# A streamed LoRA matmul: idle matmuls around TensorE's loop, a pause that waits on another store, and other chunk sizes

## The chip, the core and the metric

The kernel runs on one core of a Trainium2 chip. The metric is device time in microseconds of one execution; three runs of the kernel before gave 162.35 to 162.37, with a median of 162.37. A separate profiled execution gives the trace. Its numbers are used for everything that is read inside the kernel, and its own time is given beside its span.

The engines' short names are: PE for TensorE's matmuls, PEld for its weight loads, DVE for VectorE, ACT for ScalarE, POOL for GpSimd, SP for the SyncE queue that issues most of the transfers here.

## The reference

`x` is 16 x 2048 x 256 in float32, that is 32,768 rows of 256. `W` is 256 x 256, `lora_A` 256 x 16, `lora_B` 16 x 256, `lora_E` has 16 values.

```python
x_flat = x.reshape(-1, in_dim)
y = x_flat @ W
lora_out = x_flat @ lora_A
lora_out = lora_out * lora_E
lora_out = lora_out @ lora_B
y = y + scale * lora_out
```

Reading `x` and writing the output are 33.55 MB each.

## The kernel before

The kernel folds the low-rank part into the weights once: `weff = W + A * E * scale @ B`, in bf16 (L149 to L167). After that it is one matmul of 32,768 rows with a 256 x 256 matrix.

**Chunks and slots.** The 256 rows of 128 partitions (one "row" below is 128 rows of `x`, 131,072 bytes) are cut into six chunks by `PLAN`: 48, 32, 48, 48, 48 and 32. A partition holds consecutive rows of `x`, so that a whole chunk is one contiguous run for each partition. Four slots in SBUF (`SLOTS`) hold a chunk each; a chunk is loaded into its slot, computed there, and its result is written over it in place and stored from it. Chunk 4 goes into chunk 0's slot and chunk 5 into chunk 1's. `PIECES` splits a chunk's load into several transfers, so that work can start on the first of them: chunk 0 into 16 and 32 rows, chunk 2 into 24 and 24.

**The transfers.** All large transfers are issued by SP, in program order: load 0's first piece, W, the rest of load 0, loads 1 to 3 (L114 to L121); then, from the loop at L210, store 0 and store 1 as soon as their chunks are computed. Behind store 1 (`AFTER`), SP waits until store 0 has landed and issues load 4, waits until store 1 has landed and issues load 5. Then come stores 2 to 5, each when its chunk is done. As SP works in order, store 2 can't be issued ahead of load 5.

**Steps.** A step is eight rows, and there are 32 (`NS`). For each step, VectorE rounds the rows to bf16 (`rounded`, L141); TensorE transposes them, two bf16 values taken as one fp32 word (`transposed`, L180); VectorE copies the transposed words from PSUM to SBUF (`copied`, L145); TensorE multiplies by `weff` in two halves of eight matmuls (`multiplied`, L191); ScalarE copies each half from PSUM into the slot (L214). All buffers between the engines are double. The orders are written out by hand: VectorE does `copied(t)` and then `rounded(t + 2)`; TensorE's loop (L201) transposes step t + 1 and then multiplies step t. So the last multiplication of a chunk comes after the first transposition of the next chunk.

**Waits.** `rounded` waits for the load that brings its rows (L135). `HOLD = {3: 1}` adds a wait at chunk 3's first step, step 16: after ten no-operations on VectorE, rounding waits until store 1 has landed (L140). Step 15's multiplication stands behind the transposition of step 16 on TensorE, and so chunk 2's last rows wait for that too.

Of the kernel before, what the change touches and what calls it, by code (L numbers as in the profile page):

```python
# [3 lines left out]

PLAN = [48, 32, 48, 48, 48, 32]

PIECES = {0: [16, 32], 2: [24, 24]}

SLOTS = [48, 32, 48, 48]
LEAD = 4  # L10
AFTER = {1: [4, 5]}

HOLD = {3: 1}

S, G = 8, 4
P = 128
# [17 lines left out]
def kernel(tc, x, W, lora_A, lora_B, lora_E, scale, out):  # L34
    nc = tc.nc
# [5 lines left out]
    KC = K // P  # L41
    assert K == M and sum(PLAN) * P == N
    starts = [sum(PLAN[:i]) * P for i in range(len(PLAN))]

    steps = [(i, r) for i, b in enumerate(PLAN) for r in range(0, b, S)]
    NS = len(steps)
    assert NS % 2 == 0

    def rows_of(flat, i):
        b, r0 = PLAN[i], starts[i]  # L50
        return flat[r0:r0 + b * P, :].rearrange("(p b) k -> p b k", b=b)

    def sbuf(name, shape, dt):
        return nc.alloc_sbuf_tensor(name, shape, dt).ap()

    def psum(name, shape, dt):
        return nc.alloc_psum_tensor(name, shape, dt).ap()

    slots = [sbuf(f"xy{s}", [P, rows, K], FP32) for s, rows in enumerate(SLOTS)]
    a_sb = sbuf("a_sb", [P, KC, R], FP32)  # L60
# [4 lines left out]
    ate = sbuf("ate", [R, KC, P], BF16)  # L65
    weff = sbuf("weff", [P, KC, M], BF16)
    ident = sbuf("ident", [P, P], FP32)

    xb = [sbuf(f"xb{k}", [P, S, K], BF16) for k in range(2)]
    words = [t[:, :, :].rearrange("p s k -> p (s k)").bitcast(FP32).rearrange("p (s w) -> p s w", s=S) for t in xb]  # L70
# [4 lines left out]
    ps_y = [psum(f"psum_y{k}", [P, G, M], FP32) for k in range(2)]  # L75
# [4 lines left out]
    s_w, s_a, s_b, s_e = (Count(nc, f"s_{k}") for k in "wabe")  # L80

    pieces = {}
    for i, b in enumerate(PLAN):
        parts = PIECES.get(i, [b])
        pieces[i] = [(sum(parts[:j]), n) for j, n in enumerate(parts)]
    s_ld = {(i, r): Count(nc, f"s_ld{i}_{r}") for i in pieces for r, n in pieces[i]}
    s_st = [Count(nc, f"s_st{i}") for i in range(len(PLAN))]
    s_id, s_set, s_v, s_t, s_m, s_y = (
        Count(nc, k) for k in ("s_id", "s_set", "s_v", "s_t", "s_m", "s_y"))


    can_m = nc.alloc_semaphore("can_m")
# [1 line left out]
    can_y = [[nc.alloc_semaphore(f"can_y{h}_{k}") for k in range(2)] for h in range(S // G)]  # L94

    def slot(i):
        return slots[i % LEAD][:, :PLAN[i], :]
# [8 lines left out]
    def spent(engine, count):  # L106
        engine.wait_ge(count.sem, count.total).then_inc(count.sem, -count.total)

    def take(sem):
        nc.tensor.wait_ge(sem, 1).then_inc(sem, -1)  # L110
# [21 lines left out]
    def rounded(t):  # L132
        i, r = steps[t]
        if (i, r) in s_ld:
            nc.vector.wait_ge(s_ld[i, r].sem, 16)  # L135
        if i in HOLD and r == 0:

            for _ in range(10):
                nc.vector.engine_nop()
            nc.vector.wait_ge(s_st[HOLD[i]].sem, 16)  # L140
        nc.vector.tensor_copy(out=xb[t % 2], in_=slot(i)[:, r:r + S, :]).then_inc(can_t[t % 2], 1)  # L141

    def copied(t):
        nc.vector.wait_ge(s_t.sem, t + 1)
        nc.vector.tensor_copy(out=xt[t % 2], in_=ps_xt[t % 2]).then_inc(can_m, 1)  # L145


    nc.vector.wait_ge(s_b.sem, 16)
# [3 lines left out]
    for c in range(KC):  # L152
# [4 lines left out]
    s_v.by(nc.vector.tensor_scalar(  # L157
        out=ate, in0=ps_at, scalar1=e_sb, scalar2=float(scale),
        op0=mybir.AluOpType.mult, op1=mybir.AluOpType.mult))
    nc.tensor.wait_ge(s_v.sem, 2)  # L160
    for c in range(KC):
        aeb_done = nc.tensor.matmul(ps_aeb[:, c, :], ate[:, c, :], b_bf, start=True, stop=True)  # L162
    s_set.by(aeb_done)
    rounded(0)
    nc.vector.wait_ge(s_w.sem, 16)
    nc.vector.wait_ge(s_set.sem, 2)
    s_v.by(nc.vector.tensor_add(out=weff, in0=w_sb, in1=ps_aeb))  # L167
    rounded(1)
    for t in range(NS):
        copied(t)  # L170
        if t + 2 < NS:
            rounded(t + 2)

    nc.vector.sem_inc(can_t[NS % 2], 1)


    def transposed(k):
        nc.tensor.wait_ge(can_t[k], 1)
        for j in range(S):
            done = nc.tensor.transpose(ps_xt[k][:, j, :], words[k][:, j, :], ident)  # L180
            if j == 1:
                done.then_inc(can_t[k], -1)
        done.then_inc(s_t.sem, 1)

    def multiplied(k):
        take(can_m)
        for h in range(S // G):
            nc.tensor.wait_ge(can_y[h][k], 1)
            for j in range(G):
                for c in range(KC):  # L190
                    done = nc.tensor.matmul(  # L191
                        ps_y[h][:, j, :], pairs[k][:, h * G + j, :, c], weff[:, c, :],
                        start=(c == 0), stop=(c == KC - 1))
                if j == 0:
                    done.then_inc(can_y[h][k], -1)
            done.then_inc(s_m.sem, 1)

    transposed(0)
    nc.tensor.wait_ge(s_v.sem, 3)

    with nc.tensor.Fori(0, NS // 2):  # L201
        for k in range(2):
            transposed(1 - k)
            multiplied(k)
    s_t.total, s_m.total = NS + 1, NS * S // G

    for h in range(S // G):
# [1 line left out]
    n = 0  # L209
    for i, r in [(i, r + g) for i, r in steps for g in range(0, S, G)]:  # L210
        n += 1
        nc.scalar.wait_ge(s_m.sem, n)
        t, h = divmod(n - 1, S // G)
# [16 lines left out]
    for count in [s_a, s_id]:  # L230
        spent(nc.tensor, count)
    spent(nc.tensor, s_v)
    for count in [s_b, s_e, s_w, s_set, s_t] + list(s_ld.values()):
        spent(nc.vector, count)
    spent(nc.scalar, s_m)
    nc.tensor.wait_ge(can_y[0][NS % 2], 1).then_inc(can_y[0][NS % 2], -1)
# [37 lines left out]
```

## Time and profile before

| | us |
|---|---|
| median of three runs | 162.37 |
| the profiled execution's own time | 162.57 |
| its span, first to last instruction | 161.3 |
| outside the span | 1.27 |
| first rounding (step 0) starts | 9.60 |
| rounding waits for load 0's second piece until | 19.58 |
| stores 0 to 5 issued at | 37.21, 47.69, 91.12, 107.07, 122.79, 133.27 |
| loads 4 and 5 issued at | 73.68, 83.38 |
| TensorE's pause | 59.68 to 84.67 |
| last engine work (ScalarE's copy) ends | 133.2 |

How to read it: a page of the profile gives the busy time of each engine over the whole span, then forty equal slices with the busy share in tenths. The DMA row is the mean busy share of the core's 16 DMA engines, and the GB/s row what they moved; the packets of this kernel are up to 48 KB long, so that short windows of the rate are coarse. PEclk is TensorE's granted clock; 1.00 is the full clock and 0.50 half of it. The table of stages gives the same for stretches that one chooses. A transfer is issued by a short instruction on its queue; the time from there to landing holds both its wait behind the transfers ahead and its own movement.

### The profile page before, as it was taken

What the parts mean: (1) busy time and instruction counts of PE and PEld (TensorE: products, weight loads), DVE (VectorE), ACT (ScalarE), POOL (GpSimd) and SP (SyncE); (2) the same over time, 40 slices, a digit from 0 to 9 for tenths busy, and PEclk for the clock granted to TensorE, in tenths of its full rate; (3) what the DMA queues carried; (4) which work ended last, traced back from release to release, by engine and by line L of the source; (5) the groups of instructions that cost most, each with busy time, mean ns of one, the idle gap of its engine ahead of it and who ended that gap; (6) DMA issues with size and microseconds to landing.
All of it is one profiled execution on the core that took longest, in us unless ns stands there. A gap on an engine that the chain in (4) does not pass through costs nothing.

```text
span 161.3 us, 1875 instructions
## 1 busy us (share of the span) xinstructions
PE 93.2 (58%) x780; PEld 83.4 (52%) x780; DVE 76.6 (48%) x67; ACT 63.2 (39%) x65; POOL 0.7 (0%) x6
## 2 busy tenths in 40 slices
PE   0149179999999980000009999999999970000000
PEld 0038058999999960000008899999999960000000
DVE  0074197898989800000039589898989500000000
ACT  0300406777768680000000577776868680000000
POOL 0100000000000000000000000000000000000000
PEclk9999978999999998555555899999999997555555
DMA  4999999999999999989999989999999999999993
GB/s 137 407 496 423 423 423 433 408 463 408 506 439 427 402 390 392 500 386 398 480 435 402 500 378 406 471 431 404 463 463 415 402 451 463 427 402 402 447 447 171
DMA packets 2370, 67.42 MB, mean 418 GB/s; under 512 B 432, under 2 KB 448, under 8 KB 576
## 3 DMA queue, kind: packets, MB, share of 16 engines
q1 hardware_dynamic: 2160, 67.37, 97.7%
q10 hardware_dynamic: 208, 0.03, 0.1%
q14 instruction: 2, 0.02, 0.0%
HBM read 33.85 MB, written 33.55 MB: 418 GB/s over the span
## 4 chain that ended last, share of the span: by engine, by line
PE 44%; DMA 22%; ACT 2%; DVE 1%; issue 0%
PE psum_y L191 29%; DMA out_dram<-xy 22%; PE psum_xt L180 14%; ACT xy L214 2%; DVE xb L141 1%
## 5 line engine op out<-in xcount | busy, mean ns | idle before, releaser
L214 ACT COPY xy<-psum_y 128x1024 f32<-128x1024 f32 x64 | 61.9, 1015 | 64.0 <-PE psum_y L191 64.0
L191 PE MATMUL psum_y<-weff,xt 128*128 128x256 bf16 x512 | 64.9, 283 | 0.1
L191 PEld LDWEIGHTS psum_y<-weff,xt 128*128 128x128 bf16 x512 | 51.8, 101 | 7.6 <-issue 0.3
L141 DVE CAST xb<-xy 128x2048 bf16<-128x2048 f32 x32 | 39.0, 1217 | 32.3 <-DMA out_dram<-xy 26.8
L180 PE MATMUL psum_xt<-ident,xb 128*128 128x128 f32 x264 | 37.1, 288 | 29.7 <-DVE xb L141 29.7
L180 PEld LDWEIGHTS psum_xt<-ident,xb 128*128 128x128 f32 x264 | 32.3, 150 | 31.3 <-DVE xb L141 30.9
L145 DVE COPY xt<-psum_xt 128x1024 f32<-128x1024 f32 x32 | 39.2, 1224 | 11.2 <-PE psum_xt L180 11.2
L153 PE MATMUL psum_xt<-ident,a_sb 128*16 128x128 f32 x2 | 0.6, 397 | 6.8 <-POOL ident L127 6.8
L149 DVE CAST b_bf<-b_sb 16x256 bf16<-16x256 f32 x1 | 0.3, 281 | 7.9 <-DMA b_sb<-in_lora_B_dram 7.9
L214 ACT ACT_TABLE_LOAD x1 | 1.3, 1283 | 6.0 <-PEq L123 6.0
L153 PEld LDWEIGHTS psum_xt<-ident,a_sb 128*16 128x16 f32 x2 | 0.1, 90 | 6.7 <-DMA a_sb<-in_lora_A_dram 6.7
L162 PE MATMUL psum_xt<-b_bf,ate 16*128 16x256 bf16 x2 | 0.6, 402 | 2.4 <-DVE ate L157 2.4
L162 PEld LDWEIGHTS psum_xt<-b_bf,ate 16*128 16x128 bf16 x2 | 0.1, 104 | 2.9 <-DVE ate L157 2.9
L157 DVE TENSOR_SCALAR ate<-psum_xt,e_sb 16x256 bf16<-16x256 f32 x1 | 0.5, 473 | 1.0 <-DMA e_sb<-in_lora_E_dram 1.0
L167 DVE TENSOR_TENSOR weff<-w_sb,psum_xt 128x512 bf16<-128x512 f32 x1 | 0.7, 669 | 0.0
L127 POOL TENSOR_SCALAR_AFFINE_SELECT ident<-ident 128x128 f32<-128x128 f32 x1 | 0.3, 292 | 0.2 <-POOL ident L125 0.2
L125 POOL MEMSET ident<- 128x128 f32 x1 | 0.2, 205 | 5.4 <-POOLq L123 5.4
L255 POOL MEMSET const-bfloat16-1.0<- 128x1 bf16 x1 | 0.1, 102 | 0.0
L255 POOL MEMSET const-uint8-127<- 128x1 uint8 x1 | 0.1, 101 | 0.0
L255 POOL MEMSET const-float32-0.0<- 128x1 f32 x1 | 0.1, 98 | 0.2 <-issue 0.2
L255 POOL MEMSET const-float32-1.0<- 128x1 f32 x1 | 0.1, 98 | 0.0
## 6 DMA issues: line engine op xcount, KB each, us to landing
out_dram<-xy SPq DMA_DIRECT2D x4, 6144.0 KB, 30.6
xy<-in_x_dram SPq DMA_DIRECT2D x3, 4096.0 KB, 24.5
xy<-in_x_dram SPq DMA_DIRECT2D x2, 6144.0 KB, 39.3
out_dram<-xy SPq DMA_DIRECT2D x2, 4096.0 KB, 31.8
xy<-in_x_dram SPq DMA_DIRECT2D x2, 3072.0 KB, 36.7
xy<-in_x_dram SPq DMA_DIRECT2D x1, 2048.0 KB, 8.4
w_sb<-in_W_dram SPq DMA_DIRECT2D x1, 256.0 KB, 8.5
a_sb<-in_lora_A_dram ACTq DMA_DIRECT2D x1, 16.0 KB, 5.7
```

The costliest lines, as they stand in the source:

```text
L127: s_id.by(nc.gpsimd.affine_select(out=ident, in_=ident, compare_op=mybir.AluOpType.not_equal, fill=1.0, base=0, pattern=[[-1, P]], channel ...
L141: nc.vector.tensor_copy(out=xb[t % 2], in_=slot(i)[:, r:r + S, :]).then_inc(can_t[t % 2], 1)
L145: nc.vector.tensor_copy(out=xt[t % 2], in_=ps_xt[t % 2]).then_inc(can_m, 1)
L149: s_v.by(nc.vector.tensor_copy(out=b_bf, in_=b_sb))
L153: at_done = nc.tensor.transpose(ps_at[:, c, :], a_sb[:, c, :], ident)
L157: s_v.by(nc.vector.tensor_scalar(out=ate, in0=ps_at, scalar1=e_sb, scalar2=float(scale), op0=mybir.AluOpType.mult, op1=mybir.AluOpType.mult))
L162: aeb_done = nc.tensor.matmul(ps_aeb[:, c, :], ate[:, c, :], b_bf, start=True, stop=True)
L167: s_v.by(nc.vector.tensor_add(out=weff, in0=w_sb, in1=ps_aeb))
L180: done = nc.tensor.transpose(ps_xt[k][:, j, :], words[k][:, j, :], ident)
L191: done = nc.tensor.matmul(ps_y[h][:, j, :], pairs[k][:, h * G + j, :, c], weff[:, c, :], start=(c == 0), stop=(c == KC - 1))
L214: y = nc.scalar.copy(out=slot(i)[:, r:r + G, :], in_=ps_y[h])
L255: nc = _bacc.Bacc("TRN2", target_bir_lowering=False, num_devices=1)
```

## The change

- `PLAN` becomes 48, 40, 40, 48, 48, 32, and the slots follow. Chunk 0 is loaded in two pieces of 24 rows, chunk 2 in one piece.
- The pause moves from chunk 3's first step (step 16) to its second (step 17), and waits for store 0 instead of store 1. There VectorE then raises a semaphore, `go`, and waits for another, `s_warm`, before it rounds.
- TensorE's loop of 16 iterations becomes an outer loop of two with an inner one of eight (16 steps). After each inner loop, TensorE waits for `go` and for a free `psum_y`, issues five idle matmuls and raises `s_warm`. The second time is after the last step, where VectorE raises `go` at the end of its work.
- One idle matmul is put ahead of the low-rank matmuls, two ahead of the first step. An idle matmul multiplies the fp32 identity with a broadcast of itself, 512 columns, into `psum_y[0]`, which nobody reads in that state.

```diff
-PLAN = [48, 32, 48, 48, 48, 32]
-PIECES = {0: [16, 32], 2: [24, 24]}
-SLOTS = [48, 32, 48, 48]
+PLAN = [48, 40, 40, 48, 48, 32]
+PIECES = {0: [24, 24]}
+SLOTS = [48, 40, 40, 48]
 LEAD = 4
 AFTER = {1: [4, 5]}
-HOLD = {3: 1}
+HOLD = 0
+WARM = 1, 2, 5
...
+    wide = ident[:, :].unsqueeze(1).to_broadcast([P, 4, P])
...
-        if i in HOLD and r == 0:
+        if t == NS // 2 + 1:
             for _ in range(10):
                 nc.vector.engine_nop()
-            nc.vector.wait_ge(s_st[HOLD[i]].sem, 16)
+            nc.vector.wait_ge(s_st[HOLD].sem, 16)
+            nc.vector.sem_inc(go, 1)
+            nc.vector.wait_ge(s_warm.sem, 1)
         nc.vector.tensor_copy(out=xb[t % 2], in_=slot(i)[:, r:r + S, :]).then_inc(can_t[t % 2], 1)
...
+    def idle(n):
+        for _ in range(n):
+            last = nc.tensor.matmul(ps_y[0][:, :2, :].rearrange("p g m -> p (g m)"), ident, wide, start=True, stop=True)
+        return last
...
+    idle(WARM[0])
     nc.tensor.wait_ge(s_v.sem, 2)
     for c in range(KC):
         aeb_done = nc.tensor.matmul(ps_aeb[:, c, :], ate[:, c, :], b_bf, start=True, stop=True)
...
     nc.vector.sem_inc(can_t[NS % 2], 1)
+    nc.vector.sem_inc(go, 1)
...
+    idle(WARM[1])
     transposed(0)
     nc.tensor.wait_ge(s_v.sem, 3)
-    with nc.tensor.Fori(0, NS // 2):
-        for k in range(2):
-            transposed(1 - k)
-            multiplied(k)
+    with nc.tensor.Fori(0, 2):
+        with nc.tensor.Fori(0, NS // 4):
+            for k in range(2):
+                transposed(1 - k)
+                multiplied(k)
+        take(go)
+        nc.tensor.wait_ge(can_y[0][0], 1)
+        idle(WARM[2]).then_inc(s_warm.sem, 1)
+    s_warm.total = 2
```

More of the change, by code (lines that the diff above doesn't have):

```diff
@@ L46 @@
     NS = len(steps)
-    assert NS % 2 == 0
+    assert NS % 4 == 0
     def rows_of(flat, i):
@@ L87 @@
     s_st = [Count(nc, f"s_st{i}") for i in range(len(PLAN))]
-    s_id, s_set, s_v, s_t, s_m, s_y = (
-        Count(nc, k) for k in ("s_id", "s_set", "s_v", "s_t", "s_m", "s_y"))
+    s_id, s_set, s_v, s_t, s_m, s_y, s_warm = (
+        Count(nc, k) for k in ("s_id", "s_set", "s_v", "s_t", "s_m", "s_y", "s_warm"))
+    go = nc.alloc_semaphore("go")
     can_m = nc.alloc_semaphore("can_m")
@@ L232 @@
     spent(nc.tensor, s_v)
-    for count in [s_b, s_e, s_w, s_set, s_t] + list(s_ld.values()):
+    for count in [s_b, s_e, s_w, s_set, s_t, s_warm] + list(s_ld.values()):
         spent(nc.vector, count)
```

## The prediction

> **What bounds the kernel now.** I read the table of engines first, then the 40 slices, the chain of waits, rates by stage, and the queue's own timeline.
>
> ```profile
> PE 93.2 (58%) x780; PEld 83.4 (52%) x780; DVE 76.6 (48%) x67; ACT 63.2 (39%) x65; POOL 0.7 (0%) x6
> ...
> PEclk9999978999999998555555899999999997555555
> DMA  4999999999999999989999989999999999999993
> ...
> DMA packets 2370, 67.42 MB, mean 418 GB/s; under 512 B 432, under 2 KB 448, under 8 KB 576
> ...
> PE 44%; DMA 22%; ACT 2%; DVE 1%; issue 0%
> ```
>
> No compute engine is busy for 60% of the span. The DMA row has a 9 in nearly every slice but the first and the last. The chain gives TensorE 44%, and that line misleads: it follows semaphores, and a transfer that lies in a queue behind other transfers shows none. The next view, busy time and rate by stage (start:end, length, busy time of PE, PEld, DVE, ACT and POOL, granted clock, DMA share, GB/s), decides it:
>
> ```profile
> 2.00:10.00 8.00, 0.86 (x4) 0.25 (x4) 1.08 (x3) 1.28 (x1) 0.50 (x2) 1.00 1.04 405
> 10.00:54.00 44.00, 39.17 (x320) 34.78 (x319) 34.38 (x31) 23.64 (x25) 0.00 (x0) 0.96 1.01 435
> 54.00:59.00 5.00, 5.00 (x48) 4.67 (x47) 2.31 (x2) 3.62 (x5) 0.00 (x0) 1.00 0.88 344
> 59.00:82.00 23.00, 0.68 (x7) 0.36 (x4) 0.00 (x0) 1.76 (x2) 0.00 (x0) 0.59 1.03 443
> 82.00:106.00 24.00, 21.33 (x170) 19.25 (x171) 19.31 (x17) 12.54 (x13) 0.00 (x0) 0.83 0.99 427
> 106.00:133.00 27.00, 26.15 (x240) 24.07 (x238) 19.56 (x17) 20.07 (x22) 0.00 (x0) 1.00 1.00 431
> 133.00:158.80 25.80, 0.00 (x0) 0.00 (x0) 0.00 (x0) 0.24 (x1) 0.00 (x0) 0.53 0.99 429
> 158.80:161.30 2.50, 0.00 (x0) 0.00 (x0) 0.00 (x0) 0.00 (x0) 0.00 (x0) 0.50 0.09 39
> ```
>
> From 2 us to 158.8 us the transfers run at 427 to 443 GB/s, whether the engines work (106 to 133) or stand still (59 to 82, 133 to 158.8). One dip stands out, 344 GB/s at 54 to 59, where the first four loads end and the first store begins. The last engine work ends at 133.2, and 28 us of stores follow. So the time is bytes over rate, plus ragged ends: 67.42 MB at 435 GB/s is 155.0 us, the first packet moves at 2.0 us, and some 4 us go to the slow start, the dip and the last, uneven 2.5 us. Whether engine work can matter is a matter of when the next transfer is queued:
>
> ```profile
> 0.94 0.38 SPq L101 DMA_DIRECT2D xy<-in_x_dram  x1
> 1.38 0.44 SPq L115 DMA_DIRECT2D w_sb<-in_W_dram  x1
> 1.87 2.95 SPq L101 DMA_DIRECT2D xy<-in_x_dram  x5
> 37.21 10.82 SPq L104 DMA_DIRECT2D out_dram<-xy  x2
> 73.68 10.04 SPq L101 DMA_DIRECT2D xy<-in_x_dram  x2
> 91.12 42.48 SPq L104 DMA_DIRECT2D out_dram<-xy  x4
> ...
> DMA to landing us min/median/max: 28.0/30.6/36.5
> ```
>
> The last line is of the six stores. A store of 6.29 MB needs 14.5 us at 435 GB/s, and the shortest took 28.0 us from issue: each lay at least 13 us behind others.
>
> **The change, part by part.** The profiled execution took 162.57 us: span 161.3 and 1.27 outside. The median of the plain runs is 162.37, 0.20 less. Sizes are in rows: one row of a chunk over 128 partitions is 131,072 bytes, 0.301 us at 435 GB/s. As a check, store 1 (32 rows) landed 9.7 us after store 0, by the waits that ended at 73.68 and 83.36; 32 x 0.301 = 9.6.
>
> *Chunks.* Bytes and order of the transfers stay. Landings in the changed kernel, estimated from rows: load 0 at 19.6 as now (where rounding waited for it), load 1 at 31.6, load 2 at 43.7, load 3 at 58.2, store 0 at 73.7 as now, store 1 (now 40 rows) at 85.7, load 4 at 100.2, load 5 at 109.8, store 2 at 121.9, store 3 at 136.4, store 4 at 150.9, store 5 at 160.5. The sixteen engines issue one load fewer, 128 packets. In the trace's packet records (which no view prints) packets of the first loads follow each other on an engine every 613 ns at 16 KB, 912 at 24, 1,214 at 32, 1,816 at 48, where 37.75 ns a KB would give 604, 906, 1,208, 1,812. So a packet costs some 4 to 9 ns by itself, and eight fewer on each engine, with the 16 KB ones gone, save 0.03 to 0.1 us. I take 0.1.
>
> *First piece 24 rows, not 16.* It lands 8 x 0.301 = 2.4 us later, so the first rounding moves from 9.60 to about 12.0, and W behind it by as much. Hidden: three steps instead of two then run before the next piece lands at 19.6, and store 0, issued at 37.2 now, comes not later than that; the queue needs it at 58.2, 20 us after.
>
> *Idle matmuls, 1 and 2 ahead of the first step.* No row has a plain fp32 matmul. By fp32 transposes (eight of 128 columns in 0.87 us at full clock, 1.57 to 1.97 at half) 512 columns cost 0.44 to 1.0 us; at double the passes, 0.87 to 2.0. I take 1.7 at half clock. The first lies between 7.4 and 9.7, where TensorE waits. The two others start at 10.3 and end by 13.7, against data ready at 13.2: at most 0.5 us (1.1 at the upper end), covered by the same 20 us. The Trainium skill's "FP8 and Floating Point Precision" (section "TensorE Precision Notes") gives true fp32 four passes; that is the upper price.
>
> *The pause.* Rounding 16 stays ahead of it, so chunk 2 is finished about 64, not 91; store 2 is queued by SP behind load 5 in any case, at 85.7 instead of 91.1, and is needed at 109.8. The wait now is on store 0 (73.7) and then on five idle matmuls, 2.2 to 10 us, so rounding 17 starts at 76 to 84 against 83.4 for rounding 16. Behind it on VectorE stands everything else, copy 16 among it. Five steps at 2.62 us (the spacing of the copies in the steady stretch) plus a start of some 3 us finish chunk 3 by 92 to 100; store 3 is needed at 121.9. Then step 22 must wait for load 4 until 100.2, a stall that takes the place of part of the pause. From there 10 steps are left: 16 steps with a cold start took 83.4 to 133.3, so 49.9 - 6 x 2.62 = 34.2 us, end at 134.4; store 4, four steps earlier, at 123.9. They are needed at 136.4 and 150.9: slack of 12 and 16 us, against 11.9 and 16 now. On the path: nothing.
>
> *Whether the clock is kept.* The clock by stage in the present pause:
>
> ```profile
> 61.00:63.00 2.00, 0.00 (x0) 0.00 (x0) 0.00 (x0) 0.00 (x0) 0.00 (x0) 1.00 1.13 492
> 63.00:65.00 2.00, 0.00 (x0) 0.00 (x0) 0.00 (x0) 0.00 (x0) 0.00 (x0) 0.50 1.16 496
> 65.00:84.00 19.00, 0.00 (x0) 0.00 (x0) 0.62 (x1) 0.00 (x0) 0.00 (x0) 0.50 1.00 433
> 84.00:90.30 6.30, 5.63 (x27) 4.64 (x28) 5.15 (x5) 1.23 (x2) 0.00 (x0) 0.50 0.94 406
> ```
>
> TensorE stopped at 59.7 and was at half clock from 63; the restart stayed there until 90.3. The Trainium skill's "TensorE: Matmul & The Clock Gate" (section "Why this matters for your kernels") says that an idle gap over some 3 us brings the half clock back; the trace agrees, 3.3 us here. By that rule the change defeats itself: what five matmuls warm is cold again in the wait for load 4. Without the page: any idle time of 3.3 us or more before 100.2 does it, and the 34.2 us above already hold a cold start.
>
> *Outer loop, go, s_warm.* Two branches and two waits, under 1 us on TensorE inside that slack. The idle matmuls after the last step run beside stores.
>
> Sum: 162.57 - 0.1 = 162.5 for the profiled execution, and 162.37 - 0.1 = 162.3 for the median.
>
> **Rivals.**
> A: TensorE is the path after all, as the 44% says. For: that line. A warm clock would then save, after the pause, 1.97 - 0.87 and 3.41 - 1.75, and at 21 to 26 us 3.53 - 1.75, about 4.5 us, giving 157.9. Against: 2.0 + 155.0 + the 0.5 from the last packet to the span's end + 1.27 is 158.8 without any of it. Chance 2%.
> B, faster: the end is set by the slowest of sixteen DMA engines. By the packet records they end between 158.9 and 160.7, mean 159.5; the late ones lost 0.3 to 1.4 us on their first packet, 0.1 to 1.0 in the dip, and up to 0.7 once at 64. A different first piece redraws the start. If the last engine came halfway to the mean: 162.37 - 0.6 = 161.8. Chance 18%.
> C, slower: engine work beside stores. One DMA engine's 48 KB packets took 93 to 126 ns longer from 106 to 133, beside stores 2 and 3, and no longer beside loads or in rest. In the changed kernel steps 17 to 21 run beside store 1. If they and the idle matmuls cover all 12 us of it, that is 6.3 packets' worth at 0.11 = 0.7 us more on that engine, less 0.1 for a shorter stretch later: 162.9. It decides if that engine ends last in plain runs too and work starts by about 78. Against: the mean rates with and without work are 431 and 429 GB/s. The Trainium skill's "SBUF — State Buffer" (section "SBUF: two separate sides") says that a DMA can't be slowed by a compute operation; then C would be nothing. Chance 20%.
> D, slower: the queue runs dry because a wait is longer than I think. Store 4 would have to be 12 us late; each microsecond beyond adds one: 163.5 or more. Chance 5%.
>
> **How the numbers follow.** About 0.2% (0.3 us) is what a measurement of this kernel tells from no change. The forecast, 162.3, has 55%. Faster by more than that: A and B, 20%. Slower: C and D, 25%. Its own range is 162.0 to 162.6. The range reaches to B's end where the slowest engine comes to 0.8 below its present time, 161.6, and to C's full price, 163.0; A, D and the tails of B lie outside.
>
> **What would show it.** Right: the DMA row full from slice 2 on, last engine work between 130 and 136 with 25 us or more of stores behind it, landing minus own time above 9 us for every store, a second pause of TensorE ending near 100 with its clock at half again. Right in part: rounding 17 between 76 and 84. Wrong: a hole in the DMA row at 58, 86, 110, 122, 136 or 151; a dip at the first store much smaller or larger than 344 GB/s over 5 us; or rates beside store 1 below 425 GB/s.

## The result

The changed kernel took 163.15 us (median of 22 runs, 162.69 to 163.51), the kernel before 162.51 in the 22 runs beside it (162.29 to 163.14; the three runs shown earlier lay at the low end of these). The ratio is 1.0035, with a 95% interval of 1.0024 to 1.0045: 0.35% slower, clear of no change. The profiled execution took 163.45 us, span 162.1.

The page of the changed kernel, busy time and slices:

```profile
PE 107.8 (66%) x806; PEld 87.7 (54%) x806; DVE 75.9 (47%) x67; ACT 63.1 (39%) x65; POOL 0.7 (0%) x6
...
DMA  5999999999999989989899998999999998999992
...
DMA 39%; PE 22%; ACT 2%; DVE 1%; issue 0%
...
L156 PE MATMUL psum_y<-ident 128*128 128x512 f32 x26 | 17.5, 828 | 10.6 <-PEq L114 10.3
```

TensorE is 14.6 us busier. The idle matmuls (L156, two records each) take 17.5 us, and the rest of its work 2.9 us less than before; its mean granted clock is 0.871, where it was 0.822. The DMA row is as full as before. The stages (start:end, length, busy time of PE, PEld, DVE, ACT, POOL, granted clock, DMA share, GB/s), cut as before:

```profile
2.00:10.00 8.00, 2.14 (x4) 0.66 (x4) 0.21 (x1) 1.28 (x1) 0.50 (x2) 1.00 0.97 382
10.00:54.00 44.00, 40.16 (x324) 34.44 (x324) 34.74 (x33) 23.47 (x25) 0.00 (x0) 1.00 1.02 440
54.00:59.00 5.00, 5.00 (x48) 4.67 (x46) 2.37 (x3) 3.61 (x5) 0.00 (x0) 1.00 0.89 334
59.00:82.00 23.00, 10.98 (x41) 5.63 (x39) 3.28 (x3) 3.76 (x4) 0.00 (x0) 0.70 1.00 434
82.00:106.00 24.00, 17.87 (x141) 15.69 (x142) 16.28 (x15) 10.32 (x11) 0.00 (x0) 0.87 1.01 434
106.00:133.00 27.00, 27.00 (x245) 24.79 (x243) 19.05 (x17) 19.48 (x21) 0.00 (x0) 0.99 0.99 428
133.00:158.80 25.80, 4.61 (x11) 1.82 (x10) 0.00 (x0) 1.14 (x2) 0.00 (x0) 0.65 1.00 432
158.80:162.10 3.30, 0.00 (x0) 0.00 (x0) 0.00 (x0) 0.00 (x0) 0.00 (x0) 0.50 0.12 50
```

From 10 to 158.8 us the rates lie within 3% of those before, some above and some below, and the dip at 54 to 59 is there again, 334 against 344 GB/s. What is longer is the last line: 3.30 us at 0.12 of the DMA engines, where it was 2.50 us at 0.09. A few DMA engines are still at work when the others have ended. The packet records of the trace, put into one chain for each of the sixteen engines, give the same in numbers:

```
end of the last packet, us        before   changed
mean of the sixteen DMA engines   159.54   159.63
second last engine                160.69   160.80
last engine                       160.74   161.62
one engine's longer store packets: number, sum of their excess
                                  14, 1.51  14, 1.35
```

A longer packet is one that took at least 0.07 us more than 37.75 ns a KB. The engine that has them is the last one in both executions.

The mean engine lost 0.09 us, and the last one 0.88. The span grew by 0.85. So in these two executions the time went to the one engine that ends last, and hardly to the transfers as a whole.

The queue and the pause came as forecast:

```profile
0.94 0.38 SPq L105 DMA_DIRECT2D xy<-in_x_dram  x1
1.38 0.43 SPq L119 DMA_DIRECT2D w_sb<-in_W_dram  x1
1.85 2.44 SPq L105 DMA_DIRECT2D xy<-in_x_dram  x4
37.27 13.45 SPq L108 DMA_DIRECT2D out_dram<-xy  x2
73.62 12.43 SPq L105 DMA_DIRECT2D xy<-in_x_dram  x2
86.09 48.41 SPq L108 DMA_DIRECT2D out_dram<-xy  x4
...
DMA to landing us min/median/max: 27.9/32.6/36.6
```

Load 4 is issued at 73.62 and store 2 at 86.09, and the shortest store again took 28 us from issue to landing: no transfer was issued late. In the pause (the same columns as the stages):

```profile
73.80:79.20 5.40, 5.40 (x7) 2.30 (x8) 0.00 (x0) 0.00 (x0) 0.00 (x0) 0.50 0.92 396
79.20:81.10 1.90, 1.84 (x5) 0.53 (x3) 0.02 (x1) 0.00 (x0) 0.00 (x0) 0.98 0.95 410
95.00:98.00 3.00, 0.97 (x9) 0.62 (x7) 0.00 (x0) 1.93 (x2) 0.00 (x0) 1.00 1.06 459
98.50:100.30 1.80, 0.00 (x0) 0.00 (x0) 0.00 (x0) 0.00 (x0) 0.00 (x0) 0.85 1.14 492
101.60:106.50 4.90, 4.89 (x23) 3.96 (x24) 4.49 (x4) 1.01 (x1) 0.00 (x0) 0.50 0.99 428
```

The same in the timeline (start, length, engine, line, operation; in brackets the idle time before it and what ended that):

```profile
73.80 7.24 PE L156 MATMUL psum_y<-ident 128*128 128x512 f32 x10 [10.32 <-PEq L114]
81.08 1.23 DVE L147 CAST xb<-xy 128x2048 bf16<-128x2048 f32 x1 [19.66 <-PE psum_y L156]
100.33 1.23 DVE L147 CAST xb<-xy 128x2048 bf16<-128x2048 f32 x1 [7.46 <-DMA xy<-in_x_dram]
101.61 1.97 PE L194 MATMUL psum_xt<-ident,xb 128*128 128x128 f32 x8 [5.64 <-DVE xb L147]
```

The five idle matmuls took 7.2 us, and the full clock was granted at 79.2, near their end. Rounding 17 followed at 81.08. TensorE then stood still from 96.0 to 101.6, because rounding waited for load 4 until 100.3. In that time half the clock came back, and step 22 started at it (eight transposes in 1.97 us).

### The profile page after: what moved, and what is told of

It is laid out like the page before. It is cut to its first block, busy times and chain, and to the rows that moved or that the text cites. A ratio compares the mean times of both kernels' runs of the same rounds, so it can differ in the third digit from the quotient of the medians.

```text
span 162.1 us, 1936 instructions
## 1 busy us (share of the span) xinstructions
PE 107.8 (66%) x806; PEld 87.7 (54%) x806; DVE 75.9 (47%) x67; ACT 63.1 (39%) x65; POOL 0.7 (0%) x6
## 4 chain that ended last, share of the span: by engine, by line
DMA 39%; PE 22%; ACT 2%; DVE 1%; issue 0%
DMA out_dram<-xy 22%; DMA xy<-in_x_dram 16%; PE psum_y L205 13%; PE psum_xt L194 7%; PE psum_y L156 3%; ACT xy L234 2%; DVE xb L147 1%
## 5 line engine op out<-in xcount | busy, mean ns | idle before, releaser
L234 ACT COPY xy<-psum_y 128x1024 f32<-128x1024 f32 x64 | 61.8, 1016 | 65.6 <-PE psum_y L205 65.6
L205 PE MATMUL psum_y<-weff,xt 128*128 128x256 bf16 x512 | 62.7, 277 | 0.9 <-PEq L114 0.5
L205 PEld LDWEIGHTS psum_y<-weff,xt 128*128 128x128 bf16 x512 | 50.7, 99 | 7.9 <-issue 1.8
L194 PE MATMUL psum_xt<-ident,xb 128*128 128x128 f32 x264 | 35.9, 282 | 8.7 <-DVE xb L147 8.7
L194 PEld LDWEIGHTS psum_xt<-ident,xb 128*128 128x128 f32 x264 | 31.2, 146 | 11.9 <-DVE xb L147 10.4
L156 PE MATMUL psum_y<-ident 128*128 128x512 f32 x26 | 17.5, 828 | 10.6 <-PEq L114 10.3
L156 PEld LDWEIGHTS psum_y<-ident 128*128 128x128 f32 x26 | 6.4, 264 | 18.1 <-issue 17.5
```

Of the source, the lines that this page charges most:

```text
L156: last = nc.tensor.matmul(ps_y[0][:, :2, :].rearrange("p g m -> p (g m)"), ident, wide, start=True, stop=True)
L205: done = nc.tensor.matmul(ps_y[h][:, j, :], pairs[k][:, h * G + j, :, c], weff[:, c, :], start=(c == 0), stop=(c == KC - 1))
L234: y = nc.scalar.copy(out=slot(i)[:, r:r + G, :], in_=ps_y[h])
```

## The experiments

Each kernel was timed in five rounds beside the kernel before on the same chip; ratios are to that, with 95% intervals. The theories: **W**, engine work beside stores slows one DMA engine; **T**, the turns of the queue between loads and stores cost, more so where engines work; **F**, the 24-row first piece gives DMA engines a worse start; **P**, the chunk change as such, by sizes or by pieces; **L**, an engine once late stays late and loses more at later turns.

### Which part of the change

**The pause on store 1 again.** `HOLD = 1` in the changed kernel.

> The changed kernel with the pause waiting on store 1 again (HOLD = 1), all else as changed. Theory W (engine work beside stores slows one DMA engine by some 6% and that engine ends last): no work beside store 1 (4 us less), but steps 17 to 31 then run from about 93 to 136 and lie 3 us longer beside stores 2 and 3, so about the time of the changed kernel, 163.0 to 163.2. Theory T (the loss sits at the turns of the queue from stores to loads and back, and is larger when engines work at that moment; in the changed kernel they work at the turn at 85 us): 0.3 to 0.5 us less than the changed kernel, 162.6 to 162.9. Theory F (the 24-row first piece gives some DMA engines a worse start): no difference from the changed kernel, 163.1.

163.18 us, ratio 1.0041 (1.0024 to 1.0058). The new place of the pause is not what costs, and the work at the turn at 85 us isn't either.

**The first piece of 16 rows again.** `PIECES = {0: [16, 32]}` in the changed kernel.

> The changed kernel with chunk 0 loaded in pieces of 16 and 32 rows as before, all else as changed. Theory F: the loss goes, 162.5 to 162.6, ratio 1.000 to 1.001. Theories W and T: no difference from the changed kernel, about 163.1, ratio 1.003 to 1.004.

163.02 us, ratio 1.0030 (1.0015 to 1.0045). F alone doesn't carry the loss.

**The chunks alone.** In the kernel before:

```diff
-PLAN = [48, 32, 48, 48, 48, 32]
-PIECES = {0: [16, 32], 2: [24, 24]}
-SLOTS = [48, 32, 48, 48]
+PLAN = [48, 40, 40, 48, 48, 32]
+PIECES = {0: [24, 24]}
+SLOTS = [48, 40, 40, 48]
```

> The kernel before with the changed chunks alone (48, 40, 40, 48, 48, 32, the first in 24 + 24 rows; the pause at step 16 on store 1, no idle matmuls, one loop). Theory F: the whole loss, 163.1, ratio 1.0035. Theory T: at the turn from store 1 to load 4 no engine works, so no loss, 162.4 to 162.6. Theory W: store 1 is 2.4 us longer, so the second half starts and ends 2.4 us later and lies as long beside stores as before, 162.4 to 162.6.

163.17 us, ratio 1.0025 (1.0003 to 1.0048). No idle matmul, no moved pause, and most of the loss is there. I had expected it under F; under T, as I had put it, it should not have been.

**All but the chunks.** The changed kernel with the three lines above turned back.

> The changed kernel with the chunks and pieces of before (48, 32, 48, 48, 48, 32; 16 + 32 and 24 + 24), and with its idle matmuls, nested loop and pause at step 17 on store 0. Theory P (the loss is the chunks', as the kernel with the changed chunks alone was 0.25% slower): no loss, ratio 0.999 to 1.001. Rival Q (the loss is also in the pause and the idle matmuls, each part costing some): 1.002 to 1.004.

162.54 us, ratio 1.0009 (0.9985 to 1.0033). The estimate is near zero; the interval by itself would still allow most of the loss. The warm TensorE below, which also has idle matmuls and the old chunks, narrows it (1.0001, 0.9984 to 1.0018).

### What of the chunks

**Sizes alone, pieces alone, each piece alone, another split.** Five kernels, each the kernel before with one of these pairs of lines:

```diff
-PLAN = [48, 32, 48, 48, 48, 32]; PIECES = {0: [16, 32], 2: [24, 24]}
+PLAN = [48, 40, 40, 48, 48, 32]; PIECES = {0: [16, 32], 2: [24, 16]}
+PLAN = [48, 32, 48, 48, 48, 32]; PIECES = {0: [24, 24]}
+PLAN = [48, 32, 48, 48, 48, 32]; PIECES = {0: [24, 24], 2: [24, 24]}
+PLAN = [48, 32, 48, 48, 48, 32]; PIECES = {0: [16, 32]}
+PLAN = [48, 48, 32, 48, 48, 32]; PIECES = {0: [16, 32], 2: [16, 16]}
```

Sizes alone:

> The kernel before with chunks of 48, 40, 40, 48, 48, 32, but with as many pieces as before (16 + 32, and the third chunk in 24 + 16). Theory P by sizes (with a 40-row store 1 ahead of it, the turn to load 4 costs single DMA engines 0.4 to 0.9 us instead of 0.2): ratio 1.002 to 1.004, and a largest loss above 0.35 us in one engine's second packet of load 4. Theory P by pieces: ratio 0.999 to 1.001.

Pieces alone, both of them:

> The kernel before with its own chunks, but with chunk 0 in 24 + 24 rows and chunk 2 in one piece: one load fewer. Theory P by pieces: ratio 1.002 to 1.004. Theory P by sizes: 0.999 to 1.001, and a largest loss of about 0.2 us in the second packets of load 4, as in the kernel before.

The first piece alone:

> The kernel before with chunk 0 in pieces of 24 + 24 rows, and nothing else. If the first piece carries the part of the loss that the pieces showed together: ratio 1.001 to 1.003, and the latest engine at 8 to 12 us is 0.8 us or more behind the mean (0.5 to 0.7 with 16 rows). Otherwise 0.999 to 1.001.

Chunk 2 in one piece alone:

> The kernel before with chunk 2 loaded in one piece, and nothing else: 64 packets of 24 KB on the engines of each half become 128 of 48 KB. If this carries the part of the loss that the pieces showed together: ratio 1.001 to 1.003. Otherwise, and by the price of a packet, 0.999 to 1.001.

Another split, 48 and 32 rows in the other order:

> The kernel before with chunks of 48, 48, 32, 48, 48, 32, pieces of 16 + 32 and 16 + 16. If the 40 KB runs are what costs (their pitch in the DRAM, or their packets): no loss, ratio 0.999 to 1.001. If it is the longer store 1 ahead of the turn, or the later turn: 1.002 to 1.005, and the largest loss in load 4's second packets over 0.35 us.

```
                             us, median  ratio
sizes alone                  162.92      1.0021  (0.9998 to 1.0043)
pieces alone, both           162.96      1.0019  (0.9993 to 1.0045)
first piece alone            163.00      1.0016  (1.0000 to 1.0032)
chunk 2 in one piece alone   162.84      1.0017  (1.0000 to 1.0035)
48, 48, 32                   162.94      1.0006  (0.9987 to 1.0025)
```

Chunk 2 in one piece means 128 packets of 48 KB in place of 256 of 24 KB. Neither theory on P wins: the sizes and each of the pieces show some 0.2%, and each of these intervals reaches 1.0000. The ratio isn't the quotient of the two medians; for 48, 48, 32 that quotient is 1.0017 (162.94 to 162.66), as much as the parts show, so this kernel is not clearly without loss. Two expected signs failed as well. With the first piece alone the latest engine was 0.75 us behind the mean when W had landed, where I wanted 0.8 or more; the kernel before had 0.74. With 48, 48, 32 single packets of load 4 lost 0.39 us, above my mark of 0.35, and the ratio was still 1.0006. So a loss in load 4's second packets is no measure of the time.

**Load 5 and store 2 issued later.** In the changed kernel, after the wait on store 1:

```diff
                 nc.sync.wait_ge(s_st[later - LEAD].sem, 16)
+                if later == 5:
+                    nc.sync.wait_ge(s_m.sem, 38)
                 load(later)
```

> The changed kernel with load 5, and store 2 behind it, issued some 5 us later (at about 90 instead of 85.7 us, SP waiting for the 38th half of a multiplication), still 8 us ahead of need. Theory T (the loss in load 4's second packets, up to 0.4 to 0.9 us on single engines, comes from the turn of the queue itself): it stays, ratio 1.003 to 1.004. Rival I (it comes from the issue of load 5 and store 2, which falls into those packets): no packet of load 4 loses over 0.1 us at 85 to 88, and the ratio falls to 1.001 to 1.002.

163.56 us, ratio 1.0053 (1.0037 to 1.0068). Two engines still lost 0.38 us in packets of load 4 that began at 87.0. The issue is not their cause, and rival I fell; holding it back bought nothing.

### What makes an engine late

**TensorE work that nobody waits for, beside the last stores.** In the kernel before, behind the loop:

```diff
+    nc.tensor.wait_ge(can_y[0][NS % 2], 1)
+    with nc.tensor.Fori(0, 10):
+        for j in range(16):
+            nc.tensor.matmul(ps_y[0][:, j % G, :], pairs[0][:, j % S, :, 0], weff[:, 0, :], start=True, stop=True)
```

> The kernel before with 160 matmuls of 256 columns added behind the last step, in a loop of ten times sixteen, into a psum tile that nobody reads: some 17.5 us of TensorE work at 133 to 151 us, where now nothing runs beside stores 3 and 4, and which no transfer waits for. Theory W: the DMA engine that is slow beside work loses another 6% of 17.5 us, up to 1.0 us, so 163.3 to 163.5 (ratio 1.005 to 1.006), with one engine's packets some 0.1 us longer in that stretch. Theories T and F: no difference from the kernel before, 162.5.

163.41 us, ratio 1.0035 (1.0016 to 1.0055). Its stages:

```profile
106.00:133.00 27.00, 26.70 (x245) 24.56 (x244) 19.24 (x17) 19.99 (x21) 0.00 (x0) 1.00 0.99 428
133.00:151.00 18.00, 16.76 (x154) 14.77 (x151) 0.00 (x0) 0.00 (x0) 0.00 (x0) 1.00 0.99 427
158.80:162.10 3.30, 0.00 (x0) 0.00 (x0) 0.00 (x0) 0.00 (x0) 0.00 (x0) 0.50 0.12 50
```

The second line is work with no one behind it: no rounding, no copies. The mean rate doesn't show it (427 against 429 before), the uneven end does, 3.30 us. One engine's longer packets went on until 148 us: 24 of them, 2.45 us in all, where the kernel before had 14 and 1.51. It ended last at 161.57, a whole microsecond after the next. W is shown: work alone, on TensorE alone, beside stores, makes the kernel longer. The 0.94 us more on that engine are the 1.0 that were expected; the time grew by about 0.6, less than the ratio of 1.005 to 1.006 that was expected. A likely reason, not tested, is that without the work that engine is not always the last.

**No pause.** `HOLD = {}` in the kernel before.

> The kernel before without its pause: chunk 3's six steps run at 60 to 76 us beside stores 0 and 1, and the next wait is for load 4, at 98. Theory W (an engine loses some 6% of the time that work lies beside stores): 16 us more there, less 3 us by an earlier end, 0.7 us more on that engine, ratio 1.003 to 1.005, and its packets longer by some 0.1 us at 60 to 76. If the pause was worth nothing: 1.000.

163.51 us, ratio 1.0069 (1.0048 to 1.0090; six runs), more than expected. Its stages:

```profile
58.00:77.00 19.00, 17.24 (x155) 15.32 (x152) 13.88 (x12) 13.25 (x14) 0.00 (x0) 1.00 0.98 422
77.00:98.00 21.00, 0.00 (x0) 0.00 (x0) 0.00 (x0) 0.25 (x1) 0.00 (x0) 0.53 0.99 428
98.00:106.00 8.00, 6.69 (x48) 5.98 (x49) 7.25 (x7) 2.54 (x3) 0.00 (x0) 0.73 1.08 459
106.00:131.20 25.20, 23.80 (x219) 21.89 (x216) 17.47 (x15) 18.65 (x20) 0.00 (x0) 1.00 0.98 422
```

The first line is chunk 3's six steps, run beside stores 0 and 1, and the second is what the pause became. The packets of one engine were 0.06 to 0.12 us longer from 57 to 76 us, and again beside stores 2 and 3. So this is what the pause of the kernel before is worth: 0.7%, for 19 us of work that it keeps away from stores, less 2 us by which work ended sooner without it. By the 6% of longer packets 0.3 to 0.5% was expected; what goes beyond is not explained.

**No computation.** Only the transfers, with each store behind its chunk's loads:

```diff
-    (everything from the identity matrix to the last clean-up)
+    for i in range(len(PLAN)):
+        for r, n in pieces[i]:
+            nc.sync.wait_ge(s_ld[i, r].sem, 16)
+        store(i)
+        for later in AFTER.get(i, []):
+            nc.sync.wait_ge(s_st[later - LEAD].sem, 16)
+            load(later)
```

> The kernel before without its computation: no work on TensorE, VectorE or ScalarE; each store waits for its chunk's loads and writes x out as it came. The transfers, their sizes and their order are those of the kernel before. Theory W: no DMA engine has packets that are longer by 6% in any stretch, the slowest engine ends some 0.5 to 1.0 us sooner, 161.6 to 162.0, ratio 0.994 to 0.997. If engine work costs the transfers nothing: 162.4 to 162.6, ratio 1.000, and the slowest engine ends where it does now.

162.33 us, ratio 0.9985 (0.9954 to 1.0017). The stages of its profiled execution (start:end, length, POOL's busy time, granted clock, DMA share, GB/s):

```profile
54.00:59.00 5.00, 0.00 (x0) 1.00 0.84 334
106.00:133.00 27.00, 0.00 (x0) 1.00 0.98 426
133.00:158.80 25.80, 0.00 (x0) 1.00 0.98 425
158.80:160.50 1.70, 0.00 (x0) 1.00 0.09 39
```

The dip at 54 to 59 is there without any work, so it belongs to the transfers. The rows of longer packets are gone, and the last engine ends at 160.19, in a last stage of 1.70 us. The median fell less than expected, and its interval holds no change: the runs scatter from 161.55 to 163.91. So the whole computation costs this kernel some 0.2%, which this interval doesn't tell from nothing, and at most 0.5%.

**Two more turns.** The kernel without computation, with load 3 behind store 0:

```diff
-        for i in range(1, LEAD):
+        for i in range(1, LEAD - 1):
             load(i)
 ...
         store(i)
+        if i == 0:
+            load(3)
```

> The kernel without computation, with store 0 queued ahead of load 3 instead of behind it: the same bytes and transfers, but two more turns of the queue (load 2 to store 0, store 0 to load 3). It leaves out the computation as the other one did. Theory T (each turn costs, a turn to stores some 0.4 us on the mean engine and up to 0.7 to 1.0 on the late ones, a turn to loads 0.05 and up to 0.6): 0.5 to 1.2 us above the kernel without computation, so 162.8 to 163.5, with the mean engine ending 0.4 to 0.6 us later. If turns cost nothing and the loss at 55 us belongs to the first store alone: 162.3, no change.

163.19 us, ratio 1.0029 (1.0010 to 1.0048): 0.86 us above the kernel without computation, with the mean engine 0.33 us later in the profiled execution (159.58 against 159.25). Both intervals are wide, and the difference of the two ratios (0.0044) is only just clear of them. So turns cost by themselves, with the same bytes and no work, if the new order of the transfers does nothing else. The mean engine lost less than the 0.4 to 0.6 us that T wanted.

**The changed sizes without computation.** `PLAN = [48, 40, 40, 48, 48, 32]`, pieces 16 + 32 and 24 + 16.

> The kernel without computation, with chunks of 48, 40, 40, 48, 48, 32 in as many pieces as before (16 + 32, 24 + 16). It leaves out the computation as the other one did. Theory P by sizes, in the transfers alone: 0.3 to 0.5 us above the kernel without computation, so 162.6 to 162.9, with the largest loss in load 4 again 0.4 us or more. If the sizes cost only together with engine work: 162.3, no change.

162.74 us, ratio 1.0001 (0.9981 to 1.0020): 0.41 us above the kernel without computation, as P by sizes wanted, but the two intervals overlap. The sign in load 4 came (0.51 us), but the kernel without computation and with the old sizes had 0.65 there, so it separates nothing. Not decided.

**One engine made late.** In the kernel before, behind the first transfer:

```diff
         load(0, pieces[0][:1])
+        flat = [t[:, :, :].rearrange("p s w -> p (s w)") for t in words + xt]
+        for j, t in enumerate(extra + flat):
+            s_x.by(nc.sync.dma_start(out=t[0:1, :1021], in_=x_flat.rearrange("(o n) k -> o (n k)", o=1)[:, j * 1024:j * 1024 + 1021]), 16)
```

> The kernel before with six loads of one partition and 4 KB each behind the first x transfer, into buffers that are not yet in use. If such a load runs on a single DMA engine, that engine is late by six times 4 KB at 37.75 ns a KB, 0.9 us, from 8 us on, and all others are as before. Theory L (the end is that of the latest engine; an engine that is late at the turns to load 4 and to store 2 loses more there than the others, 0.2 to 0.3 us each against 0.07): that engine is among the last two at the end, and the time is 0.4 to 1.4 us above the kernel before, ratio 1.003 to 1.008. If lateness were made up for or did not matter (the transfers share a common limit): ratio 1.000 to 1.001.

162.66 us, ratio 1.0003 (0.9990 to 1.0015). The six loads did run one behind the other on one engine, from 7.57 to 8.53 us. That engine had been the first of all to finish the first x piece (7.56; the mean was 7.88). In the profiled execution it ended last, at 160.83 us, level with the engine that was slow beside stores (160.81). So half of L is right, in this one trace: an engine made late at 8 us is still late at 160. The price was wrong, and by the time alone the other forecast (1.000 to 1.001) came true. A likely reason, not tested: the delay went to an engine that was ahead, and with two late engines the end is no later than with one.

### Less work beside stores

**A warm TensorE after the old pause.** The changed kernel with the old chunks, `WARM = 1, 2, 8`, and at step 17:

```diff
-            nc.vector.wait_ge(s_st[HOLD].sem, 16)
-            nc.vector.sem_inc(go, 1)
-            nc.vector.wait_ge(s_warm.sem, 1)
+            nc.vector.wait_ge(s_st[0].sem, 16)
+            nc.vector.sem_inc(go, 1)
+            nc.vector.wait_ge(s_st[1].sem, 16)
```

> The changed kernel with the chunks and pieces of before, the pause at step 17 until store 1 has landed, and eight idle matmuls on TensorE between the landing of store 0 and that of store 1, which rounding doesn't wait for. So step 16 is already done when the second half starts at 83.4, and TensorE is at full clock then. Theory W: work beside stores 2 and 3 ends some 5 to 6 us sooner (one step of 2.6, a cold start of 3); at 0.06 to 0.08 us a microsecond (the 6% of the packets, and 1.1 us for 13 to 16 us without the pause) that is 0.3 to 0.45 us less than the kernel before, ratio 0.997 to 0.998. If idle matmuls cost the store 1 beside them as much as other work: 8 us of them take it back, ratio 0.999 to 1.001.

162.70 us, ratio 1.0001 (0.9984 to 1.0018). The warming works, as its timeline shows (start, length, engine, line, operation):

```profile
73.55 9.21 PE L156 MATMUL psum_y<-ident 128*128 128x512 f32 x16 [8.88 <-PEq L114]
83.13 1.23 DVE L147 CAST xb<-xy 128x2048 bf16<-128x2048 f32 x1 [21.89 <-DMA out_dram<-xy]
...
84.42 1.10 PE L194 MATMUL psum_xt<-ident,xb 128*128 128x128 f32 x8 [1.66 <-DVE xb L147]
85.64 1.91 PE L205 MATMUL psum_y<-weff,xt 128*128 128x256 bf16 x16
```

The kernel before at the same place:

```profile
84.67 1.97 PE L180 MATMUL psum_xt<-ident,xb 128*128 128x128 f32 x8 [24.99 <-DVE xb L141]
86.43 3.62 PE L191 MATMUL psum_y<-weff,xt 128*128 128x256 bf16 x16
```

The idle matmuls end before the second half starts, its first transposes take 1.10 us instead of 1.97, and the first 16 matmuls 1.91 instead of 3.62. Work ended only 3.6 us sooner (the last copy at 129.66 instead of 133.25) and not 5 to 6: rounding 22 stood 3.0 us waiting for load 4, until 97.95. As the idle matmuls stand in the loop, eight more of them ran behind the last step, from 128.8 us, beside stores. The engine that is slow beside stores did gain what was expected: 11 longer store packets with 1.18 us of excess, where the kernel before had 14 with 1.51. The time is the same. In the profiled execution another engine ended last, at 161.55, after a loss of 1.09 us at the turn to store 2; the one that is slow beside stores ended at 160.54. Expected were 0.3 to 0.45 us less; the interval allows 0.26. So the gain in time didn't come. No kernel with the full computation was measurably faster than the kernel before.

**The pause one step later.** In the kernel before:

```diff
-        if i in HOLD and r == 0:
+        if i in HOLD and r == S:
```

> The kernel before with its pause one step later (at step 17 instead of 16, still until store 1 has landed), and nothing else. Theory W: one step of 2.6 us less beside stores 2 and 3, and one step more beside store 0, so no difference: ratio 0.999 to 1.001.

162.63 us, ratio 0.9998 (0.9975 to 1.0021). As expected, nothing.

## Why the prediction was wrong

**The time.** 162.3 was forecast with a range to 163.0, and 163.15 was measured. Of the 0.85 between, 0.14 is the kernel before itself, whose median beside the changed kernel was 162.51 and not 162.37. The rest is the 0.1 that I took as a gain, and some 0.6 of loss.

**The step that failed is the chunks, costed at a gain of 0.1 us** ("Bytes and order of the transfers stay", "I take 0.1"), together with the first piece, which was called hidden. In the two profiled executions the mean DMA engine moved by no more than 0.09 us. But the sum was made for the mean engine, and the span ends with the last one. The runs sort by the chunks, in groups that were made after the results were known. Five kernels with the full computation have neither a 40-row chunk, nor a 24-row first piece, nor a 48-row chunk 2 in one piece (all but the chunks; 48, 48, 32; the late engine; the warm TensorE; the pause one step later): ratios of 0.9998 to 1.0009, mean 1.0003, two of them with idle matmuls. Nine kernels have one or more of the three, the changed kernel among them: 1.0016 to 1.0053, mean 1.0029, with the moved pause and without. By these ratios the two groups don't overlap, though the gap between them, 1.0009 to 1.0016, is smaller than one kernel's interval, and by the quotient of its medians the kernel with 48, 48, 32 (1.0017) would stand among the nine. The case rests on the kernels that differ most: the changed chunks alone lose 1.0025 (1.0003 to 1.0048), and the two kernels with idle matmuls and old chunks 1.0009 and 1.0001.

What in the chunks makes the last engine later is not settled: each part shows some 0.2% that its own interval doesn't clear, and no run confirmed a mechanism. In the two profiled executions the last engine lost 0.39 us more in the dip at 55 us (load 3's last packet) and 0.38 more in load 4's second packet, and no more beside stores. That is one execution each, and the kernel with 48, 48, 32 shows such losses in load 4 with a ratio of only 1.0006. In the kernel with the chunks alone a different engine ended last, at 161.62, with losses at the dip, in store 0, in load 4 and at the turn to store 2 and none from work beside stores; the engine that is slow beside stores ended at 160.73. Over one profiled execution of each kernel, the mean engine ended at 159.52 on average in the kernel before and the five, and at 159.68 in the nine; the last engine at 161.19 and 161.57. So a smaller part of the loss may lie with all engines.

**What bounds the kernel** was right: the transfers, not TensorE. Without any computation the time is at most 0.5% shorter. Rival A fell: TensorE had 14.6 us more to do and a second cold start, and no transfer was issued after its turn in the queue.

**The timeline** was right where the queue depends on it. Rounding 17 was forecast at 76 to 84 and came at 81.1, load 4 was forecast at 100.2 and rounding went on at 100.3, the last store was forecast at 134.4 and issued at 134.17, and the second restart was at half clock as forecast. Rival D fell with it: the shortest store waited as long as before.

Two steps of it were wrong and cost nothing. Chunk 3 was to be finished by 92 to 100, and store 3 was issued at 107.93: step 21 is multiplied behind the transposition of step 22, which waited for load 4. It was needed only at 121.9. The two idle matmuls ahead of the first step were to start at 10.3 and to end by 13.7, and they ran from 12.72 to 16.3, 3 us past the data and not 0.5. Their price was nearly right (some 1.8 us each, 1.7 forecast); they began late because the low-rank matmuls ahead of them did, at 12.19 instead of 9.73, as lora_E landed later. Store 0 was still issued at 37.27, where it was 37.21.

One sign of being wrong came up and means little: the rate beside store 1 is 421 GB/s from 73.7 to 85.7 us, under the 425 that the prediction named. The kernel before has 417 GB/s from 62 to 73.7 with no engine at work, so windows of this length scatter by as much.

**Rival C had the sign and a true mechanism, but not the cause.** One DMA engine does lose some 6% while engines work beside stores; the added work at the end and the missing pause both show it. But in the changed kernel that loss is 1.35 us, against 1.51 before: step 17 began at 81 us, when store 1 was nearly through, and the seven us of idle matmuls in the pause, ten records in all, left no longer packets. The condition that C named, work from about 78 on, was not met.

**Rival B** named the right place, the slowest of sixteen engines and a redrawn start, and let it go one way only. A redraw can go up as well; it should have stood on both sides.

**The range** shifted one engine by what was known of it. The kernel before scatters by 0.85 us over 22 runs, and three runs that agree within 0.02 had hidden that.

## What to carry to other kernels

When all sixteen DMA engines are busy to the end, the time is that of the last one: build a chain of packets for each engine and look at the spread, since neither the mean rate nor the chain of waits shows it. An edit that leaves bytes and order alone can still make the last one later, and here that was the only part of the edit with a measurable effect. Keep engine work away from stores where there is a choice, and don't take three runs that agree closely for the scatter of a kernel whose end is set by the latest of sixteen.

## What the runs showed of the hardware

- Beside stores, engine work made one DMA engine's packets some 6% longer (48 KB in 1.92 instead of 1.815 us), and beside loads not at all, at the same work. TensorE alone suffices. The Trainium skill's "SBUF — State Buffer" (section "SBUF: two separate sides") says that a DMA can't be slowed by a compute operation; for fifteen engines the traces agree, for one they do not. Dense short instructions did it (160 matmuls of 256 columns in 17 us), five long ones of 512 columns in the 7 us of the pause did not (beside the five behind the last step, two packets took 0.06 us longer). What that engine shares with the instructions, and whether the recording of the trace has a part in it, was not tested.
- The first turn of the queue from loads to stores (load 3 to store 0) cost the mean engine 0.2 to 0.7 us, with work or without; the second (load 5 to store 2) cost it less, under 0.3. Two more turns made the kernel without computation 0.86 us longer.
- Over the twenty traces, engines that began load 4 over 0.3 us behind the mean lost 0.20 us in it (the sum of what its packets took over the shortest of their size), against 0.04 for the others; in load 5, just before the turn to store 2, 0.25 against 0.05. In load 3 the difference is small against the loss itself (0.54 and 0.45). This was read from the traces, and no run forced it.
- The granted clock fell 3.3 us after TensorE stopped in the pause before, and 2.1 and 3.8 us after it stopped in the two of the changed kernel (63.5 to 65.6, 96.0 to 99.8). The idle matmuls needed 5.4 us to raise it (73.8 to 79.2), and 4.2 in the kernel with the warm TensorE (73.55 to 77.79). They warmed five steps, and the next wait undid it.
